# A two-layer diffusion block with routed experts: four edits between the output projection and the first expert

## The chip, the cores and the metric

The kernel runs on one core of one Trainium2 chip. The metric is the device time of one execution, in microseconds (us); the time before is the median of three runs. Engine names in this text: PE is TensorE's matmul side and PEld its weight loads, DVE is VectorE, ACT is ScalarE, POOL is GpSimd, SP is the queue that issues nearly all DMAs.

## The reference, cut to what matters

256 latent tokens `x` and 256 context tokens `ctx`, 1024 wide, pass two layers. Each layer has mixers whose merged result goes through one output projection, and then a mixture of 16 experts in which every expert takes its 32 best tokens per stream:

```python
x = x + g1 * merge_branches(attn_x, conv_x, pool_x, gate_x, lp)      # ends with  (...) @ lp['w_out']
x = x + g2 * expert_choice_ffn(modulate(rmsnorm(x, norm2_g[l]), sh2, sc2), w_router[l], w_e_gate[l], ...)
# expert_choice_ffn, per stream:
aff = softmax(h @ w_router)                      # (N, 16)
g, idx = top_k(aff.T, 32)                        # each expert's 32 tokens
xe = h[idx]
ye = (silu(xe @ w_gate) * (xe @ w_up)) @ w_down * g
out = zeros.at[idx].add(ye)
```

In layer 0 both streams go through the experts (64 tokens an expert), in layer 1 only `x` does (32 tokens an expert). The experts' weights are fp32, 12.6 MB an expert, 16 experts, two layers: some 400 MB of the 530 MB that the kernel reads.

## The kernel before

Everything is traced by the tile framework: the program is a list of instructions in Python order, and a planner reorders them by priority, readiness and estimated cost into one fixed instruction list for each engine. Each engine then runs its list strictly in order, so an instruction that waits holds all those behind it.

**The output projection**, `project(s)` (L846 on), for stream `s`: two halves `nh` of 512 output columns. For each half two PSUM banks, `pss[0]` and `pss[1]`, one for each 128 tokens (`t`). The weights come in four quarters `k2`; `split` (L229 on) makes a high part on ACT (L238) and a low part (L239: on POOL in layer 0, on DVE in layer 1), in one of two `ws` buffers. A quarter is 12 products (L872): three steps `st` (high x high, low x high weights, high x low weights), two `kk`, two `t`. After the last quarter, for each `t`, DVE multiplies by the gate (`tmp`, L877), the residual addition into `XS` follows (L879: on POOL for `nh` 1, `t` 0, otherwise on DVE), and ACT takes the squares (L880).

**The router**, `route(s)` (L884 on), a generator that is advanced in pieces. It turns `XS` into columns by PE transposes (L895), four to a bank, copies the bank out (L899 on ACT or L901 on DVE, in turn), multiplies by the router weights (L904), then comes the serial part: logits (L912 to L921), softmax, 32 best by four rounds of maximum and replace on DVE (L942, L943), slots, and the 0/1 selection matrix `S` (L965, L968), made for the last stream in chunks of four experts. Its first half of transposes needs only the projection's first column half and runs within the second.

**The gather**, `gather(s, parts)` (L979 on): for each of 8 column blocks `d` two fp32 products (L987) of `XS` (128 x 128, the weights of the array) with `S` (32 columns for each expert of the part), and an evacuation on DVE or ACT (L994, L992). Each product stands in the trace as two matmuls and two weight loads. In layer 0 `gather(0, 1)` is one part for stream 0 and overlaps `route(1)`; `gather(NS - 1, 4)` serves the last stream in four parts of four experts, of which the first runs ahead of expert 0.

**The experts** (L1033 on): for each of 16, gate and up products (L1080) in four steps `i`, then SiLU and product (L1085, L1087), then 8 or 16 steps of the gather of a later part (L1090), transposes (L1095), the down products (L1103 in layer 0, L1108 in layer 1), and every 4th (layer 0) or 2nd (layer 1) expert the scatter (L1125).

**The weights' stream**: SP issues the expert weights in pieces of 2 MB (L355) in a fixed order into slots (`order`). Each slot carries an older tile, and the DMA waits until that tile was last read. In layer 1 the first 11 entries hold expert 0 and most of expert 1. Of these the pieces in the memory of the projection's weight buffers are issued as the projection ends, the half piece in `xc` is issued when expert 0's step 0 was read, and the piece in `W01` after these when expert 1's step 0 was read. In layer 0 four entries are taken out of the later part of the order (`del order[77:81]`).

Of the kernel before, what the change touches and what calls it, by code (L numbers as in the profile page):

```python
# [121 lines left out]
def paired(c):  # L122

    return slice(256 * (c // 2) + c % 2, 256 * (c // 2) + 256, 2)
# [3 lines left out]
def dit_block(ctx: ExitStack, tc: tile.TileContext, out, kcv, kb16, rope_in, tok, cols, w_mod0, w_mod,  # L128
# [16 lines left out]
    def bank(tag, dt=F32):  # L145
        pool, bufs = psum[tag]
        return pool.tile([128, 512], dt, tag=tag, name=tag, bufs=bufs)
# [19 lines left out]
    def t2(name, n=512, dt=F32):  # L167
        return L.tile([128, n], dt, tag="t2", name=name, bufs=6)
# [42 lines left out]
    for l in range(DEPTH):  # L211
# [634 lines left out]
        def project(s):  # L846
            ssq[s] = small([128, 2, 2], "ssq")
            gbs = []
            for nh in range(2):
                gb = t2("gb")  # L850
                rr = 32 * nh + 16 * s
                pg = bank("ax")
                nc.tensor.matmul(pg, ident[:, rr:rr + 1].to_broadcast([128, 128]), GM[l], start=True,
                                 stop=True)
                nc.scalar.activation(gb, pg, AF.Copy)
                gbs.append(gb)
            for nh in range(2):
                pss = [bank("mm"), bank("mm")]
                for k2 in range(4):
                    if k2 % 2 == 0:  # L860
                        wo = load(w_out[l, nh, k2 // 2], "p (k n) -> p k n", k=4)
                    ws = split(wo[:, 2 * (k2 % 2):2 * (k2 % 2) + 2, :], "p (k n) -> p k n",
                               LOW["wout"][l], k=2)
                    wh, wl = [v.rearrange("p (k n) -> p k n", k=2) for v in ws]
                    for st in range(3):
                        for kk in range(2):
                            k = 2 * k2 + kk
                            for t in range(2):
                                tok = slice(256 * s + 128 * t, 256 * s + 128 * t + 128)
                                a = (mh, ml, mh)[st][:, k, tok]  # L870
                                b = (wh, wh, wl)[st][:, kk, :]
                                nc.tensor.matmul(pss[t], a, b, start=k == 0 and st == 0,  # L872
                                                 stop=k == 7 and st == 2)
                    yield
                for t in range(2):
                    tmp = t2("tmp")
                    nc.vector.tensor_mul(tmp, pss[t], gbs[nh])  # L877
                    xs = XS[s][:, t, nh * 512:(nh + 1) * 512]
                    (nc.gpsimd if nh == 1 and t == 0 else nc.vector).tensor_add(xs, xs, tmp)  # L879
                    nc.scalar.activation(t2("junk", 512, BF16), xs, AF.Square,  # L880
                                         accum_out=ssq[s][:, nh, t:t + 1])
                yield

        def route(s):  # L884
            pl = bank("ax")
            for d in range(8):
                nc.tensor.matmul(pl[32 * (d % 4):32 * (d % 4) + 32, 256:384], wr[:, d, :],
                                 modT[l][:, 1, s, 8 + d:9 + d].to_broadcast([128, 128]),
                                 start=d < 4, stop=d >= 4)
            for d2 in range(4):  # L890
                pt = bank("ax")
                for dd in range(2):
                    for t in range(2):
                        d = 2 * d2 + dd
                        nc.tensor.transpose(pt[:, dd * 256 + t * 128:dd * 256 + t * 128 + 128],  # L895
                                            XS[s][:, t, paired(d)], ident)
                xT = t2("xT")
                if d2 % 2:
                    nc.scalar.activation(xT, pt, AF.Copy)  # L899
                else:  # L900
                    nc.vector.tensor_copy(xT, pt)  # L901
                for dd in range(2):
                    d = 2 * d2 + dd
                    nc.tensor.matmul(pl[32 * (d % 4):32 * (d % 4) + 32, 0:256], wra[:, s, d, :],  # L904
                                     xT[:, dd * 256:dd * 256 + 256], start=d < 4, stop=d >= 4)
                if d2 % 2:
                    yield
            ss = small([128, 2], "ss")
            nc.gpsimd.tensor_add(ss, ssq[s][:, 0], ssq[s][:, 1])
            r = rms_scale(ss, 2)  # L910
# [65 lines left out]
            yield  # L976


        def gather(s, parts):  # L979
            ne = NE // parts  # L980
            for part in range(parts):
                es = slice(ne * part, ne * part + ne)
                for d in range(8):
                    px = bank("mm")[:, :32 * ne]
                    for t in range(2):
# [27 lines left out]
            pass  # L1013
        if NS == 2:
            xeT = [big(q, "xeT").rearrange("p (k e c) -> p k e c", k=4, e=NE) for q in "CD"]
            ga = gather(0, 1)
            for _ in rt1:
                next(ga, None)
                next(ga, None)
            for _ in ga:  # L1020
                pass
        else:
            xe = big("C", "xeT").rearrange("p (k e c) -> p k e c", k=8, e=NE)
            xeT = [xe[:, 0:4], xe[:, 4:8]]
        ga = gather(NS - 1, 4)
        for _ in range(8):
            next(ga)

# [4 lines left out]
        for e in range(NE):  # L1033
# [49 lines left out]
            for f in range(nb):  # L1083
# [2 lines left out]
                hm = t2("hm")  # L1086
                nc.vector.tensor_mul(hm[0:64, :], si[0:64, :], pgu[f][64:128, :])  # L1087
                hs.append(hm)
            for _ in range(8 if e == 0 or NS == 2 else 16):
                next(ga, None)  # L1090
            pt = bank("ax")
            for f in range(nb):
# [107 lines left out]
```

## Time and profile before

| | |
|---|---|
| median of 3 runs | 1712.94 us (1711.73 to 1713.78) |
| the profiled execution's own time | 1712.34 us |
| its span, first to last instruction | 1710.5 us |
| PE busy | 1483.2 us, 87% |
| DVE busy | 670.3 us, 39% |
| ACT busy | 407.6 us, 24% |
| POOL busy | 232.4 us, 14% |
| DMA, mean | 310 GB/s, 530 MB |

The profile is of one execution. Its page gives the span in 40 slices of 42.76 us with the rate of the DMAs in each; a rate near 428 GB/s is the highest that any long stretch reaches. "Granted clock" is the share of TensorE's 2.4 GHz: 1.00 is 2.4 GHz and 0.50 is 1.2 GHz. "Idle before <- X" in a row of the timeline is how long the engine stood before this instruction, and what ended the wait.

### The profile page before, as it was taken

Reading aid. Unit: us, or ns where it says so; the run is one execution under the profiler, and the core shown is the slowest. Engines: PE = TensorE matmul, PEld = TensorE weight load, DVE = VectorE, ACT = ScalarE, POOL = GpSimd, SP = SyncE. Lnnn points to the kernel's source line nnn. Section 1 sums busy time; section 2 is a strip of 40 time slices with the busy share of each in tenths; the row PEclk is TensorE's granted clock in tenths of the full one; section 3 lists DMA queues with packets and bytes.
Section 4 is the critical chain, followed back from the end, with each engine's and each line's share of the span. In section 5 each row is a group of like instructions: output and inputs, shape, how many; then the busy total and the mean of one; then the engine's idle time right before and its main releaser. Section 6 shows DMA issues by size and latency. Waiting matters only on the chain. (4 is left out here: it accounts for less than half of the span.)

```text
span 1710.5 us, 19121 instructions
## 1 busy us (share of the span) xinstructions
PE 1483.2 (87%) x7788; PEld 802.1 (47%) x7788; DVE 670.3 (39%) x1137; ACT 407.6 (24%) x760; POOL 232.4 (14%) x234
## 2 busy tenths in 40 slices
PE   6999989999999999999998899999979765666575
PEld 3665667888654433333332267789844111111111
DVE  3568993352553221121211268975542110111011
ACT  3455312232432100000000257434421000000001
POOL 0300430154740000000000020325100000000000
PEclk9999999999999999999999999999989887878878
DMA  9643435234546999999999865566689999999996
GB/s 398 230 173 130 148 144 207 75 139 181 197 176 255 425 428 427 428 426 428 428 407 428 334 242 179 196 225 229 268 336 429 427 429 427 428 427 428 428 428 258
DMA packets 48185, 530.01 MB, mean 310 GB/s; under 512 B 5345, under 2 KB 6113, under 8 KB 7906
## 3 DMA queue, kind: packets, MB, share of 16 engines
q1 hardware_dynamic: 46224, 526.10, 75.8%
q10 hardware_dynamic: 1874, 2.70, 0.5%
q8 instruction: 61, 1.00, 0.2%
q14 instruction: 26, 0.21, 0.0%
HBM read 527.73 MB, written 1.05 MB: 309 GB/s over the span
## 5 line engine op out<-in xcount | busy, mean ns | idle before, releaser
L1080 PE MATMUL mm<-we,xeT 128*32 128x512 f32 (+1 forms) x1880 | 347.1, 662 | 97.8 <-DMA we<-in_w_e_dram 97.8
L1080 PEld LDWEIGHTS mm<-we,xeT 128*32 128x32 f32 (+1 forms) x1880 | 95.1, 129 | 337.5 <-issue 190.2
L496 PE MATMUL mm<-hh,ws 128*128 128x512 f32 (+1 forms) x672 | 221.8, 349 | 0.3
L497 PE MATMUL mm<-hl,ws 128*128 128x512 f32 (+1 forms) x672 | 218.6, 344 | 0.5 <-DVE hl L430 0.4
L238 ACT ACTIVATE ws<-w 128x1024 fp32r<-128x1024 f32 x132 | 139.3, 1058 | 303.6 <-PE mm L499 202.5
L1087 DVE TENSOR_TENSOR hm<-si,mm 64x512 f32<-64x512 f32 x48 | 33.1, 690 | 405.8 <-ACT si L1085 271.4
L1085 ACT ACTIVATE si<-mm 64x512 f32<-64x512 f32 x48 | 28.3, 590 | 684.9 <-PE mm L1080 684.9
L478 DVE SCALAR_TENSOR_TENSOR acc<-up,dw,acc 128x512 f32<-128x512 f32 (+1 forms) x240 | 156.7, 693 | 1.1
L239 DVE TENSOR_TENSOR ws<-w,ws 128x1024 fp32r<-128x1024 f32 x94 | 122.3, 1304 | 70.5 <-ACT ws L238 70.2
L496 PEld LDWEIGHTS mm<-hh,ws 128*128 128x128 f32 x672 | 127.3, 190 | 29.2 <-issue 12.6
L497 PEld LDWEIGHTS mm<-hl,ws 128*128 128x128 f32 x672 | 127.4, 190 | 18.6 <-issue 3.5
L499 PE MATMUL mm<-hh,ws 128*128 128x512 f32 (+1 forms) x672 | 132.7, 339 | 1.0 <-DVE ws L239 0.9
L239 POOL TENSOR_TENSOR ws<-w,ws 128x1024 fp32r<-128x1024 f32 x38 | 97.2, 2564 | 211.2 <-ACT ws L238 211.2
L1103 PE MATMUL mm<-we,hT 128*64 128x512 f32 x432 | 111.2, 639 | 5.0 <-ACT hT L1098 4.8
L499 PEld LDWEIGHTS mm<-hh,ws 128*128 128x128 f32 x672 | 107.1, 189 | 15.9 <-DVE ws L239 2.1
L1045 POOL COPY sel<-kc 48x128 f32<-48x128 f32 (+1 forms) x16 | 4.6, 285 | 799.8 <-DVE hm L1087 428.8
L1115 DVE TENSOR_TENSOR Y<-mm,G 32x512 f32<-32x512 f32 x64 | 44.0, 687 | 135.8 <-PE mm L1103 135.0
L1108 PE MATMUL mm<-we,hT 128*32 128x512 f32 x424 | 69.1, 762 | 11.6 <-DMA we<-in_w_e_dram 9.6
L1103 PEld LDWEIGHTS mm<-we,hT 128*64 128x64 f32 x432 | 33.5, 146 | 76.5 <-issue 66.1
L1125 PE MATMUL ax<-Y,sg 128*128 128x512 f32 x128 | 58.4, 603 | 8.8 <-DVE Y L1118 6.4
L1118 DVE TENSOR_TENSOR Y<-mm,G 64x512 f32<-64x512 f32 x32 | 22.0, 688 | 96.1 <-PE mm L1108 95.7
L1095 PE MATMUL ax<-kc,hm 64*128 64x64 f32 x192 | 32.6, 294 | 31.0 <-DVE hm L1087 30.2
(260 smaller groups left out, 1715.3 us busy)
## 6 DMA issues: line engine op xcount, KB each, us to landing
we<-in_w_e_dram SPq DMA_DIRECT2D x166, 2048.0 KB, 26.6
w<-in_w_mod_dram SPq DMA_DIRECT2D x44, 1024.0 KB, 5.3
w<-in_w_in_dram SPq DMA_DIRECT2D x42, 1024.0 KB, 4.9
A<-in_w_e_dram SPq DMA_DIRECT2D x20, 2048.0 KB, 23.2
w<-in_w_out_dram SPq DMA_DIRECT2D x12, 1024.0 KB, 4.9
we<-in_w_e_dram SPq DMA_DIRECT2D x10, 1024.0 KB, 17.3
wm<-in_w_mod_dram SPq DMA_DIRECT2D x4, 1024.0 KB, 18.0
w<-in_w_attn_o_dram SPq DMA_DIRECT2D x4, 1024.0 KB, 4.9
```

The costliest lines, as they stand in the source:

```text
L238: nc.scalar.activation(h, src, AF.Copy)
L239: (nc.gpsimd if eng == "p" else nc.vector).tensor_sub(lw, src, h.bitcast(F32))
L478: nc.vector.scalar_tensor_tensor(acc[:, ch], up[:, ch, :, k:k + 256], dw[:, 4 * k + ch:4 * k + ch + 1], acc[:, ch], op0=ALU.mult, op1=ALU.add)
L496: nc.tensor.matmul(ps, wh[:, k, :], ah[:, k, :n], start=k == 0, stop=False)
L497: nc.tensor.matmul(ps, wh[:, k, :], al[:, k, :n], start=False, stop=False)
L499: nc.tensor.matmul(ps, wl[:, k, :], ah[:, k, :n], start=False, stop=k == nk - 1)
L1080: nc.tensor.matmul(o, xeT[k // 4][:, k % 4, e, :], w[:, kk, 512 * f:512 * f + 512], start=k == 0, stop=k == 7)
L1087: nc.vector.tensor_mul(hm[0:64, :], si[0:64, :], pgu[f][64:128, :])
L1103: nc.tensor.matmul(pd[64 * h:64 * h + 64, :], hT[:, 64 * k:64 * k + 64], rhs, start=k == 0, stop=k == 7)
L1108: nc.tensor.matmul(pd[o:o + 32, :], hT[:, c0:c0 + 32], rhs, start=k < 2, stop=k >= 6)
L1115: nc.vector.tensor_mul(Y[b0:b0 + 32, s, cols], pd[rw, :], G2[l][rw, :])
L1125: nc.tensor.matmul(po, sgs[s][:, t * 128:(t + 1) * 128], Y[:, s, cols], start=True, stop=True)
```

## The change

Four edits. In the projection's last quarter (`k2` 3) the 12 products are sorted by `t`, so that all six of `t` 0 come before the six of `t` 1. The addition L879 is on DVE in every case. The router's transposes are made in two halves of four column blocks, within a half by `t` first, into two banks, whose copies go to DVE and to ACT. And the last stream's gather is cut 2, 2, 4, 4, 4 experts instead of 4, 4, 4, 4; in layer 1 expert 0 now advances it by 16 steps instead of 8.

```diff
--- before.py
+++ after.py
@@ -862,21 +862,21 @@
                     ws = split(wo[:, 2 * (k2 % 2):2 * (k2 % 2) + 2, :], "p (k n) -> p k n",
                                LOW["wout"][l], k=2)
                     wh, wl = [v.rearrange("p (k n) -> p k n", k=2) for v in ws]
-                    for st in range(3):
-                        for kk in range(2):
-                            k = 2 * k2 + kk
-                            for t in range(2):
-                                tok = slice(256 * s + 128 * t, 256 * s + 128 * t + 128)
-                                a = (mh, ml, mh)[st][:, k, tok]
-                                b = (wh, wh, wl)[st][:, kk, :]
-                                nc.tensor.matmul(pss[t], a, b, start=k == 0 and st == 0,
-                                                 stop=k == 7 and st == 2)
+                    steps = [(st, kk, t) for st in range(3) for kk in range(2) for t in range(2)]
+                    if k2 == 3:
+
+                        steps.sort(key=lambda q: q[2])
+                    for st, kk, t in steps:
+                        k = 2 * k2 + kk
+                        tok = slice(256 * s + 128 * t, 256 * s + 128 * t + 128)
+                        nc.tensor.matmul(pss[t], (mh, ml, mh)[st][:, k, tok], (wh, wh, wl)[st][:, kk, :],
+                                         start=k == 0 and st == 0, stop=k == 7 and st == 2)
                     yield
                 for t in range(2):
                     tmp = t2("tmp")
                     nc.vector.tensor_mul(tmp, pss[t], gbs[nh])
                     xs = XS[s][:, t, nh * 512:(nh + 1) * 512]
-                    (nc.gpsimd if nh == 1 and t == 0 else nc.vector).tensor_add(xs, xs, tmp)
+                    nc.vector.tensor_add(xs, xs, tmp)
                     nc.scalar.activation(t2("junk", 512, BF16), xs, AF.Square,
                                          accum_out=ssq[s][:, nh, t:t + 1])
                 yield
@@ -887,24 +887,22 @@
                 nc.tensor.matmul(pl[32 * (d % 4):32 * (d % 4) + 32, 256:384], wr[:, d, :],
                                  modT[l][:, 1, s, 8 + d:9 + d].to_broadcast([128, 128]),
                                  start=d < 4, stop=d >= 4)
-            for d2 in range(4):
-                pt = bank("ax")
-                for dd in range(2):
-                    for t in range(2):
-                        d = 2 * d2 + dd
-                        nc.tensor.transpose(pt[:, dd * 256 + t * 128:dd * 256 + t * 128 + 128],
-                                            XS[s][:, t, paired(d)], ident)
-                xT = t2("xT")
-                if d2 % 2:
-                    nc.scalar.activation(xT, pt, AF.Copy)
-                else:
-                    nc.vector.tensor_copy(xT, pt)
-                for dd in range(2):
-                    d = 2 * d2 + dd
-                    nc.tensor.matmul(pl[32 * (d % 4):32 * (d % 4) + 32, 0:256], wra[:, s, d, :],
-                                     xT[:, dd * 256:dd * 256 + 256], start=d < 4, stop=d >= 4)
-                if d2 % 2:
-                    yield
+            for h in range(2):
+
+                pts = [bank("ax"), bank("ax")]
+                for t in range(2):
+                    for dd in range(4):
+                        o = 256 * (dd % 2) + 128 * t
+                        nc.tensor.transpose(pts[dd // 2][:, o:o + 128], XS[s][:, t, paired(4 * h + dd)],
+                                            ident)
+                xT = [t2("xT"), t2("xT")]
+                nc.vector.tensor_copy(xT[0], pts[0])
+                nc.scalar.activation(xT[1], pts[1], AF.Copy)
+                for dd in range(4):
+                    nc.tensor.matmul(pl[32 * dd:32 * dd + 32, 0:256], wra[:, s, 4 * h + dd, :],
+                                     xT[dd // 2][:, 256 * (dd % 2):256 * (dd % 2) + 256],
+                                     start=h == 0, stop=h == 1)
+                yield
             ss = small([128, 2], "ss")
             nc.gpsimd.tensor_add(ss, ssq[s][:, 0], ssq[s][:, 1])
             r = rms_scale(ss, 2)
@@ -976,10 +974,11 @@
             yield
 
 
-        def gather(s, parts):
-            ne = NE // parts
-            for part in range(parts):
-                es = slice(ne * part, ne * part + ne)
+        def gather(s, sizes):
+            e0 = 0
+            for ne in sizes:
+                es = slice(e0, e0 + ne)
+                e0 += ne
                 for d in range(8):
                     px = bank("mm")[:, :32 * ne]
                     for t in range(2):
@@ -1013,7 +1012,7 @@
             pass
         if NS == 2:
             xeT = [big(q, "xeT").rearrange("p (k e c) -> p k e c", k=4, e=NE) for q in "CD"]
-            ga = gather(0, 1)
+            ga = gather(0, (16,))
             for _ in rt1:
                 next(ga, None)
                 next(ga, None)
@@ -1022,7 +1021,7 @@
         else:
             xe = big("C", "xeT").rearrange("p (k e c) -> p k e c", k=8, e=NE)
             xeT = [xe[:, 0:4], xe[:, 4:8]]
-        ga = gather(NS - 1, 4)
+        ga = gather(NS - 1, (2, 2, 4, 4, 4))
         for _ in range(8):
             next(ga)
 
@@ -1086,7 +1085,7 @@
                 hm = t2("hm")
                 nc.vector.tensor_mul(hm[0:64, :], si[0:64, :], pgu[f][64:128, :])
                 hs.append(hm)
-            for _ in range(8 if e == 0 or NS == 2 else 16):
+            for _ in range(8 if NS == 2 else 16):
                 next(ga, None)
             pt = bank("ax")
             for f in range(nb):
```

## Rows read from the trace of the kernel before

**Rows 1.** The page: GB/s moved by DMA in the 40 slices.

```profile
GB/s 398 230 173 130 148 144 207 75 139 181 197 176 255 425 428 427 428 426 428 428 407 428 334 242 179 196 225 229 268 336 429 427 429 427 428 427 428 428 428 258
```

**Rows 2.** The chain of work that ended last: start, us, what.

```profile
1339.66 39.37 DMA we<-in_w_e_dram
```

**Rows 3.** Windows: stretch, length, busy PE PEld DVE ACT POOL, clock, DMA share, GB/s.

```profile
1268.00:1272.00 4.00, 4.00 (x44) 1.22 (x40) 0.00 (x0) 0.00 (x0) 0.00 (x0) 1.00 0.45 129
1284.00:1288.00 4.00, 4.00 (x44) 1.27 (x40) 0.00 (x0) 0.00 (x0) 0.00 (x0) 1.00 1.01 434
```

**Rows 4.** Timeline of SP's issues, layer 1: start, us, what.

```profile
1269.17 0.33 SPq L355 DMA_DIRECT2D we<-in_w_e_dram  x1
...
1285.56 0.33 SPq L355 DMA_DIRECT2D we<-in_w_e_dram  x1
```

**Rows 5.** Timeline, layer 1, from the projection's end to the router's products.

```profile
1242.94 1.07 PE L872 MATMUL mm<-ws,ml 128*128 128x512 f32 x4
1243.85 1.07 PE L872 MATMUL mm<-ws,mh 128*128 128x512 f32 x4
1244.73 1.29 DVE L877 TENSOR_TENSOR tmp<-mm,gb 128x512 f32<-128x512 f32 x2 [2.91 <-PE mm L872]
1245.50 1.26 POOL L879 TENSOR_TENSOR xr<-xr,tmp 128x512 f32<-128x512 f32 x1 [24.88 <-DVE tmp L877]
1246.05 1.26 DVE L879 TENSOR_TENSOR xr<-xr,tmp 128x512 f32<-128x512 f32 x1
...
1248.39 0.60 ACT L899 ACTIVATE xT<-ax 128x512 f32<-128x512 f32 x1 [0.26 <-PE ax L895]
1248.78 1.33 PE L904 MATMUL ax<-xT,rt 128*32 128x256 f32 x8 [0.42 <-DVE xT L901]
```

**Rows 6.** Gather and 64-column transposes at both clocks (timeline; windows as Rows 3).

```profile
518.68 4.04 PE L987 MATMUL mm<-S,xc 128*128 128x128 f32 x32 [1.32 <-ACT S L968]
...
1260.00:1264.00 4.00, 3.42 (x15) 2.93 (x16) 2.63 (x11) 2.90 (x9) 0.00 (x0) 0.50 1.04 446
1261.10 6.17 PE L987 MATMUL mm<-S,xr 128*128 128x128 f32 x32 [0.58 <-ACT S L968]
1278.47 0.55 PEld L1095 LDWEIGHTS ax<-kc,hm 64*128 64x128 f32 x4
...
1481.00:1482.00 1.00, 0.39 (x3) 0.39 (x4) 0.56 (x1) 0.00 (x0) 0.00 (x0) 0.50 1.00 426
1481.61 0.55 PEld L1095 LDWEIGHTS ax<-kc,hm 64*128 64x128 f32 x4 [3.21 <-DVE hm L1087]
```

**Rows 7.** Layer 0: two issues of SP, one PE wait, one window as Rows 3.

```profile
553.32 0.33 SPq L355 DMA_DIRECT2D we<-in_w_e_dram  x1
...
833.19 3.65 PE L1080 MATMUL mm<-we,xeT 128*64 128x512 f32 x16 [0.87 <-DMA we<-in_w_e_dram]
...
878.22 0.33 SPq L355 DMA_DIRECT2D we<-in_w_e_dram  x1
880.00:888.00 8.00, 8.00 (x40) 2.70 (x38) 2.74 (x4) 0.00 (x0) 0.00 (x0) 1.00 0.95 360
```

**Rows 8.** Layer 0, expert 3 (no gather beside it): timeline of PE.

```profile
618.71 1.48 PE L1095 MATMUL ax<-kc,hm 64*128 64x64 f32 x8 [0.63 <-DVE hm L1087]
620.94 5.25 PE L1103 MATMUL mm<-A,hT 128*64 128x512 f32 x16 [0.75 <-ACT hT L1098]
626.02 3.60 PE L1103 MATMUL mm<-we,hT 128*64 128x512 f32 x16
```

**Rows 9.** Layer 0, projection to gather: timeline, L879 (min/median/max ns), window as Rows 3.

```profile
L879 DVE TENSOR_TENSOR xr<-xr,tmp x6: 692/976/2249, 451.4 to 1246.1; 128x512 f32<-128x512 f32 x6
...
495.43 2.40 POOL L239 TENSOR_TENSOR ws<-w,ws 128x1024 fp32r<-128x1024 f32 x1 [3.00 <-ACT ws L238]
497.66 1.07 PE L872 MATMUL mm<-ws,ml 128*128 128x512 f32 x4
499.60:518.70 19.10, 17.39 (x62) 7.67 (x60) 12.94 (x37) 6.05 (x13) 2.37 (x4) 1.00 0.50 208
```

## The prediction

> **What bounds the kernel now.** I read the page's strip of DMA rates first. From slice 13 to 21 and again from slice 30 on it stands at 407 to 430 GB/s, which is all that these engines move [rows 1]: through most of both expert stages the kernel waits for weights. The chain of waits says the same, as its last third is one transfer after the other [rows 2]. So an edit that makes the router or the first gather shorter pays only if it moves the moment from which the weights stream without a break. I therefore looked for the last break in each layer, and for the release that ends it.
>
> Layer 1: the stream stands still around 1270, where 129 of 428 GB/s were moved in 4 us, a loss of 4 x (1 - 129/428) = 2.8 us [rows 3]. It resumes when expert 0's first step frees a half slot at 1269.17 [rows 4]; counted as full rate from 1270.8 on, an issue takes 1.65 us to become traffic. Four transfers of 7.3 MB follow. At 417 to 428 GB/s they last to about 1288.1. The next one waits for expert 1's first step and is issued at 1285.56 [rows 4], so it counts from 1287.2: in time, with some 0.9 us to spare, and the window there is full at 434 [rows 3].
>
> Layer 0: the stream is continuous from the issue at 553.32 (expert 1's first step). One later break stands out: the window 880 to 888 moved 360 GB/s, after an issue that a down product of PE released at 878.22 [rows 7]. That is a loss of 8 x (1 - 360/428) = 1.3 us. Until then PE ran from 520 on with one wait for weights, 0.87 us at 833 [rows 7]. At that place PE sets the stream, not the other way round.
>
> **Part by part.**
>
> *Last quarter by token halves.* It adds no product. Four products take 0.91 us (1242.94 to 1243.85 [rows 5]), one 0.23. With `t` 0 first its bank is ready 6 x 0.23 = 1.4 us before the end, where now it is one product before. Three costs. The low part of the weights is needed after four products, not eight, 0.9 us earlier. In layer 0 POOL finishes it at 495.43 + 2.40 = 497.83, and it would be wanted at 497.66 [rows 9], so PE stalls 0.2 us there. In layer 1 DVE makes it in half that time and I cost it at nothing; without that cover it is at most 0.9. And the last product that reads `ml` comes two products later, which delays the first transfers after the projection by 0.45 us; the later release (below) hides that.
>
> *Additions on DVE.* In layer 1 the serial tail now is: products end 1244.92, two gate products 1.29, POOL's addition 1.26 from 1245.50, DVE's stretched to 1.26 beside it until 1247.31, copies to 1248.99, router products 1.33 from 1248.78 to 1250.11 [rows 5]. After: `t` 0 is multiplied and added (0.65 + 0.69) inside the cover of the six products of `t` 1. Then 0.65 + 0.69 for `t` 1, to about 1246.4; four transposes, 0.7; the two copies side by side behind ACT's squares, to 1248.0; router products 0.64 at full clock, to 1248.6. That is 1.5 us earlier, with bounds of 0.7 (additions alone) and 2.0. The gain on POOL is nothing, since POOL is idle there.
>
> In layer 0 the same addition meets POOL at work on splits of the next stream at the end of `project(0)`: DVE's L879 took 692 ns alone and up to 2249 beside POOL [rows 9]. POOL's addition takes 1.26 and keeps the splits away while it runs. Two serial additions of up to 2.2 delay `route(0)`, behind whose steps PE's list holds `project(1)`: 0 to 1 us, I take 0.4. At the end of `project(1)` no split is left and the gain is as in layer 1, but the path then shares PE with 32 long matmuls of `gather(0)`. PE is busy 17.39 of the 19.10 us from there to the first gather of stream 1 [rows 9], so at most 1.7 us can go; I take 1.0, with bounds of 0 and 1.7.
>
> *Transposes by halves.* The same 16 transposes and four copies for each stream; its gain is in the tail above. Both copies of a half now stand together, so two `ax` banks and two `xT` buffers are held at a time. Of four and six that is room enough, and I cost it at nothing, or 0.7 (one copy) if a bank is missing.
>
> *First gather for two experts.* This is the disputed price, since no 64-column gather is in the trace. At full clock a part of four takes 4.04 us for 32 loads and 32 matmuls, 0.126 a pair; at half clock 6.17 in layer 1, mostly 0.21 a pair [rows 6]. If columns set the pace, a half part takes half. If the load of 128 weight columns does, nothing is won at full clock. The nearest rows are L1095's: loads of 128 columns beside matmuls of 64, four in 0.55 us at full clock and four in 0.55 at half clock [rows 6], 0.12 to 0.14 each. So I take 32 x 0.12 + 0.15 = 4.0 us for a part of two at either clock. Layer 0 wins 0 to 0.3 (0.2), layer 1 wins 2.2 on the first part. The price is a fifth part of 4.0 us on PE.
>
> The Trainium skill, "TensorE: Matmul & The Clock Gate", section "LDWEIGHTS (loading the stationary operand)", gives the load as columns / 1.2 ns whatever the rows, 107 ns for 128; by that a part of two could not go under 32 x 0.107 = 3.4 us, and the rows above sit a little over it.
>
> *Where the fifth part lands, layer 1.* Expert 0 now pulls two parts (4.0 + 4.1) before its down products instead of one (4.1). Expert 1's first step, which ends the stream's next wait, moves by -1.5 (tail) - 2.2 (first part) + 4.0 (extra part) + 0 to 1.2 (2.35 us of expert 0's products at half clock, as the first part no longer outlasts the slow stretch) = +0.3 to +1.5, middle +0.9. The break at 1270 does close: step 0 ends some 3 us earlier. But the stream, 2.3 us ahead, then stands at `W01`: its shift is -0.9 + 0.9 = 0, with bounds of -1.2 and +0.7. The gain is given back one slot later. I take -0.1.
>
> *Where it lands, layer 0.* Expert 1's first step comes G = 1.0 + 0.2 - 0.4 = 0.8 us earlier, and so does the stream. Expert 3 now carries a part that it did not have: +4.1 on PE. It fills a stall of 0.63 and may save the slow stretch that followed, 5.25 against 3.60 for the same 16 matmuls, 1.65 [rows 8]. So the net is +1.8 to +3.5; I take 2.3, near the lower end, since the part keeps PE busy just where it fell idle. PE had 0.87 of waiting at 833 to absorb it. The release at 878 moves by -0.8 + 2.3 - 0.87 = +0.6, with bounds of -1.1 (G of 2.0, the stretch saved) and +3.6 (G of -1.0, the stretch kept).
>
> The sum on the profiled execution, 1712.34: +0.6 - 0.1 = +0.5, so 1712.8. The median of the runs lies 0.6 above that execution: **1713.4 us**.
>
> **The rivals.**
>
> *Columns set the gather's pace.* Then the first two parts of layer 0 take 2.0 us each and the total gather work stays what it was. The release at 878 then moves by -1.0 + 0.4 - (0.6 to 2.3 saved in expert 3) - 0.87, some -2.9. In layer 1 expert 1's step moves by -1.5 - 3.1 + 2.0 + 0.5 = -2.1, and the stream wins all of 2.3. Sum -5.2: **1707.7**. For it speaks only that the half-clock part was paced by columns; against it L1095's rows, the same at both clocks.
>
> The same page of the Trainium skill has a rule for this side in "Back-to-back issue gap": N / 2.4 + 2.5 ns for an isolated stream, 29 ns at 64 columns, which would halve the gather; L1095's 0.12 to 0.14 us for 64 columns speaks against its use here.
>
> *The lists fall well.* The planner's new order lets `project(1)` end 1.5 us earlier (against the 0.4 later that I take), the tail of layer 0 gives its full 1.7, and expert 3's slow stretch is saved: G is 3.4, layer 0 -3.4 + 1.8 - 0.87 = -2.5, layer 1 -1.0. Sum -3.5: **1709.4**.
>
> *Slower: DVE's additions beside POOL's splits.* If both additions of `project(0)` meet a split (from some 3 us of overlap on this decides), `route(0)` comes 1.5 to 2.5 us later, PE's list waits behind it, and `project(1)` ends 2 us later. With the tail's 1.0 and 0.2 G is -0.8. Expert 3 keeps its slow stretch, +3.5. Layer 0: +0.8 + 3.5 - 0.87 = +3.4, layer 1 +0.4. Sum +3.8: **1716.7**. For it: 2249 ns in rows of this very line. Against it: the earlier start of `t` 0 may let its addition pass between two splits.
>
> **How the numbers follow.** About 0.2%, 3.4 us, is what a measurement of this kernel can tell from no change: 1709.5 to 1716.4. No change to speak of (1710.5 to 1715.8): 0.68. Columns: 0.07. Lists fall well: 0.12, half of it beyond the bound. Slower by additions and the extra part: 0.13, most of it beyond. So faster 0.14, same 0.74, slower 0.12. The range reaches into the rivals on both sides: 1708.6 to 1716.8.
>
> **What would show it.** Part of two: a first L987 group of 3.8 to 4.2 us in both layers; one of 2.0 to 2.5 makes the column rival right. Tail: 1.2 to 1.8 us less between the last L872 and L904 in layer 1, and no L879 on POOL. Break at 1270 gone, and a new one of 1 to 2.5 us where SP waits for expert 1's step near 1286: without it layer 1 gains up to 2.3 and I am wrong there. Layer 0: L879 on DVE near 466 at 2.2 us, expert 3 with an L987 group, and SP's late release near 878 later relative to 553. What I can't see from here is the planner's new order of each engine's list. If it moves the gather's extra part behind expert 0's down products, or the stream's issues, the sum changes by up to 3 us either way.

## The result

The changed kernel takes **1727.08 us** (median of 4 runs, 1723.45 to 1727.87) against 1713.36 for the kernel before beside it: a ratio of **1.0077, 95% interval 1.0056 to 1.0098**. It is 13.7 us slower. The forecast was 1713.4, with a range up to 1716.8 and a chance of 0.12 for slower.

The profiled execution has a span of 1724.5 us, 14.1 more than before. The products of layer 1's projection begin at 1220.00 before and at 1230.04 after: layer 0 costs 10.0 us, layer 1 another 4.0.

First the strips of the page after: granted clock in tenths, and the rate of the DMAs. In slice 12 (517 to 561 us here, 513 to 556 before) the rate is 185 GB/s, where before it was 255 [rows 1]; in slice 30 it is 390, where before it was 429.

```profile
PEclk9999999999998999999999999999979878887778
...
GB/s 397 227 171 129 147 150 198 88 154 161 184 174 185 428 428 428 427 427 429 426 407 430 352 251 176 177 232 237 266 335 390 429 426 430 426 429 426 429 426 263
```

PE around the first experts of layer 0, timeline of the kernel after (start, us, line, operation, matmuls in the row, wait before):

```profile
520.75 5.16 PE L986 MATMUL mm<-S,xc 128*128 128x64 f32 x32 [1.32 <-ACT S L966]
525.85 15.99 PE L1079 MATMUL mm<-we,xeT 128*64 128x512 f32 x64
541.77 4.12 PE L986 MATMUL mm<-S,xc 128*128 128x64 f32 x28
545.82 0.57 PE L1094 MATMUL ax<-kc,hm 64*128 64x64 f32 x3
546.32 0.69 PE L986 MATMUL mm<-S,xc 128*128 128x64 f32 x4
546.93 0.86 PE L1094 MATMUL ax<-kc,hm 64*128 64x64 f32 x5
548.53 6.29 PE L1102 MATMUL mm<-A,hT 128*64 128x512 f32 x16 [0.74 <-ACT hT L1097]
554.65 3.60 PE L1102 MATMUL mm<-we,hT 128*64 128x512 f32 x16
558.09 4.46 PE L1079 MATMUL mm<-we,xeT 128*64 128x512 f32 x20
```

And the same stretches as windows (busy PE, PEld, DVE, ACT, POOL, then the granted clock, DMA share, GB/s):

```profile
520.00:523.00 3.00, 2.25 (x19) 2.25 (x20) 2.31 (x10) 2.70 (x10) 0.00 (x0) 1.00 0.00 0
523.00:527.00 4.00, 4.00 (x19) 3.26 (x20) 0.69 (x2) 1.14 (x4) 0.00 (x0) 0.52 0.00 0
527.00:530.00 3.00, 3.00 (x8) 0.71 (x6) 0.00 (x0) 0.00 (x0) 0.00 (x0) 0.50 0.00 0
...
546.00:550.00 4.00, 3.25 (x16) 2.00 (x18) 0.27 (x1) 1.00 (x2) 0.00 (x0) 0.63 0.49 209
550.00:554.00 4.00, 4.00 (x12) 1.18 (x10) 0.00 (x0) 0.00 (x0) 0.00 (x0) 0.52 0.00 0
554.00:558.00 4.00, 4.00 (x20) 1.26 (x18) 0.00 (x0) 0.00 (x0) 0.00 (x0) 1.00 0.55 143
```

Read the two together. The first part of two begins at 2.4 GHz, and PE has no wait from 520.75 on; yet from 523.2 the clock is 1.2 GHz, and expert 0's first products run at that. The part takes 5.16 us, where the part of four took 4.04 [rows 6]. The second part ends the same way: at 547.0, as its last products run and with no wait of PE since 520.75, the clock falls again, and 16 down products take 6.29 us, while the next 16 take 3.60. Expert 1 starts at 558.09, before at 549.68. In the last column the weights' stream stands at 0 from 550 to 554; finer windows have 16 GB/s from 549 on and nothing until 555.

SP's list shows why it stopped so long. Three pieces go out, and the next entry is the load into slot A, which waits for the slow down products; the entry behind it had its slot free from about 542 on (in `e3_piece_order`, below, that piece goes out at 542.15):

```profile
531.58 7.20 SPq L355 DMA_DIRECT2D we<-in_w_e_dram  x3
554.87 0.33 SPq L355 DMA_DIRECT2D A<-in_w_e_dram  x1
555.24 6.82 SPq L355 DMA_DIRECT2D we<-in_w_e_dram  x2
```

Before, a fourth piece was issued at 536.64, ahead of slot A's load at 546.46. The planner exchanged the two entries.

In layer 1, PE's timeline and windows of the kernel after:

```profile
1269.17 7.09 PE L986 MATMUL mm<-S,xr 128*128 128x64 f32 x32 [0.57 <-ACT S L966]
1276.19 1.06 PE L1079 MATMUL mm<-we,xeT 128*32 128x512 f32 x1
...
1285.52 2.75 PE L986 MATMUL mm<-S,xr 128*128 128x64 f32 x20
1288.70 5.45 PE L986 MATMUL mm<-S,xr 128*128 128x64 f32 x44 [0.44 <-DVE xeT L993]
```

```profile
1272.00:1276.00 4.00, 4.00 (x20) 4.00 (x20) 1.03 (x3) 0.81 (x2) 0.00 (x0) 0.50 0.97 418
1276.00:1280.00 4.00, 4.00 (x22) 1.07 (x25) 0.00 (x0) 0.40 (x1) 0.00 (x0) 0.50 0.62 254
1280.00:1284.00 4.00, 4.00 (x36) 1.04 (x32) 0.00 (x0) 0.00 (x0) 0.00 (x0) 0.89 0.79 268
...
1296.00:1300.00 4.00, 4.00 (x40) 1.17 (x36) 0.48 (x1) 0.31 (x1) 0.00 (x0) 1.00 0.75 311
1300.00:1304.00 4.00, 4.00 (x44) 1.23 (x40) 0.00 (x0) 0.00 (x0) 0.00 (x0) 1.00 0.49 127
```

The half part takes 7.09 us, more than the whole part's 6.17 [rows 6]: 20 loads fill 4.00 us at 1.2 GHz, 0.2 each, and loads (PEld) are as busy as products. At that clock a pair takes 0.213 us from start to start in both kernels; the whole part was shorter because the clock came back at 1265.9, 4.8 us after it began. Here PE is without a wait from 1269.17, but the clock comes back only at 1280.9, well into expert 0's products. Against 428 GB/s the four windows with low rates lost 1.6 + 1.5 + 1.1 + 2.8 = 7.0 us of stream, where before the break at 1270 lost 2.8 [rows 3]. The difference, 4.2, is the 4.0 us of layer 1.

### The profile page after: what moved, and what is told of

Same layout as the page of the kernel before. It is cut to its first block, busy times and chain, and to the rows that moved or that the text cites. A ratio compares the mean times of both kernels' runs of the same rounds, so it can differ in the third digit from the quotient of the medians.

```text
span 1724.5 us, 19262 instructions
## 1 busy us (share of the span) xinstructions
PE 1501.4 (87%) x7852; PEld 813.4 (47%) x7852; DVE 675.4 (39%) x1148; ACT 410.9 (24%) x768; POOL 226.3 (13%) x231
## 5 line engine op out<-in xcount | busy, mean ns | idle before, releaser
L1079 PE MATMUL mm<-we,xeT 128*32 128x512 f32 (+1 forms) x1880 | 352.0, 668 | 95.1 <-DMA we<-in_w_e_dram 95.1
L1094 PE MATMUL ax<-kc,hm 64*128 64x64 f32 x192 | 32.6, 297 | 30.3 <-DVE hm L1086 29.8
```

What stands on the lines that cost most here:

```text
L1079: nc.tensor.matmul(o, xeT[k // 4][:, k % 4, e, :], w[:, kk, 512 * f:512 * f + 512], start=k == 0, stop=k == 7)
```

## The experiments

The theory after this reading: products of 64 columns behind weight loads of 128 are no shorter than those of 128 columns, **and they bring the array's clock down or keep it down**, so that the expert's products behind them run at half speed. Rivals: SP's exchanged entries; the additions on DVE and the planner's new lists around the projection; the fifth part by itself. Each comparison is with runs of the kernel before on the same chip, in five rounds. The times are medians; the ratio comes from all the runs and is not that of the medians. `e1` to `e4` ran on one chip, `e5` to `e7`, `e8` and `e9`, and `e10` to `e12` on three others, on which the kernel before had medians of 1713.18, 1714.29, 1712.92 and 1713.56; between two groups only distances from the kernel before are compared.

| kernel | us | against before (95%) | projection of layer 1 begins | from there to the end of the span |
|---|---|---|---|---|
| before (profile) | | | 1220.00 | 490.5 |
| after | 1727.08 | 1.0077 (1.0056 to 1.0098) | 1230.04 | 494.5 |
| `e1_no_fifth` | 1711.84 | 0.9985 (0.9973 to 0.9998) | 1221.35 | 489.5 |
| `e2_fifth_in_layer1` | 1719.19 | 1.0029 (1.0017 to 1.0040) | 1222.29 | 496.8 |
| `e3_piece_order` | 1722.98 | 1.0049 (1.0032 to 1.0067) | 1227.47 | 494.3 |
| `e4_full_columns` | 1712.29 | 0.9994 (0.9983 to 1.0005) | 1218.94 | 491.1 |
| `e5_full_columns_layer0` | 1710.15 | 0.9979 (0.9970 to 0.9989) | 1219.60 | 489.2 |
| `e6_pool_addition_kept` | 1711.09 | 0.9989 (0.9980 to 0.9999) | 1221.48 | 489.6 |
| `e7_warm_before_narrow` | 1716.74 | 1.0010 (0.9999 to 1.0020) | 1220.60 | 495.1 |
| `e8_fifth_wide_alone` | 1711.99 | 0.9991 (0.9982 to 0.9999) | 1219.27 | 490.6 |
| `e9_old_transposes` | 1710.99 | 0.9985 (0.9976 to 0.9995) | 1222.12 | 489.3 |
| `e10_changed_beside` | 1725.79 | 1.0075 (1.0063 to 1.0088) | 1228.23 | 494.3 |
| `e11_piece_order_beside` | 1722.28 | 1.0048 (1.0036 to 1.0060) | 1224.73 | 495.6 |
| `e12_narrow_layer0` | 1717.22 | 1.0021 (1.0008 to 1.0034) | 1227.11 | 490.3 |

### Without the fourth edit

```diff
-        ga = gather(NS - 1, (2, 2, 4, 4, 4))
+        ga = gather(NS - 1, (4, 4, 4, 4))
...
-            for _ in range(8 if NS == 2 else 16):
+            for _ in range(8 if e == 0 or NS == 2 else 16):
```

> The change without its fourth edit: the last stream's gather is again 4, 4, 4, 4 experts, the other three edits stay. Theory 'narrow parts' (the two parts of 64 columns cost more than parts of 128, and the array falls to 1.2 GHz after them): most of the 13.7 us is gone; what is left is layer 0's projection, which ended 2.6 us later, against a tail that is some 2 us shorter in layer 1 and pays nothing because of the next release: 1712 to 1716. Rival 'projection and router' (additions on DVE beside POOL's splits, transposes by halves, and the planner's new lists from them): 1722 to 1727. No slow stretch of the clock at the first experts of layer 0 by the first theory.

1711.84 us: the whole loss is gone, and 0.15% is won. The fourth edit holds all of it; the rival around the projection falls.

### The fourth edit in one layer

```diff
-        ga = gather(NS - 1, (2, 2, 4, 4, 4))
+        ga = gather(NS - 1, (4, 4, 4, 4) if NS == 2 else (2, 2, 4, 4, 4))
```

> The whole change, but the gather of layer 0 stays at four parts of four; only layer 1 has 2, 2, 4, 4, 4. Theory 'narrow parts': layer 0 costs as much as without the fourth edit, layer 1 adds the 4 us that it adds in the changed kernel: 3 to 5 us over the run without the fourth edit, 1716 to 1720. Rival 'everything is in layer 0' (layer 1 hides it behind the weights): the same time as without the fourth edit, within 1 us.

1719.19: 7.4 us over `e1_no_fifth`, more than the 3 to 5 expected. Layer 1 hides nothing of it. This profile has one slow stretch more than that of the changed kernel, inside the second narrow part. PE's one wait there is 0.44 us, at 1280.48, and the clock falls at 1282.1; 44 products take 6.97 us, where the changed kernel's took 5.45:

```profile
1278.00:1280.00 2.00, 2.00 (x16) 1.80 (x15) 0.69 (x2) 1.94 (x4) 0.00 (x0) 1.00 1.01 410
1280.00:1284.00 4.00, 3.56 (x23) 3.52 (x23) 1.79 (x4) 0.94 (x3) 0.00 (x0) 0.76 0.99 420
```

For layer 0 the tuple is the other way round, and SP's entries are put back as in the next experiment:

> The three first edits, five parts with two of 64 columns in layer 0 alone, four parts in layer 1, and SP's order as in the kernel before. It isolates what narrow parts cost in layer 0. If the costs add up (1711.8 without the fourth edit, 6.1 us between the traces with and without narrow parts at layer 1's start): 1716 to 1719. Rival 'the expert stage of layer 0 takes the delay back before layer 1': within 2 us of 1711.8.

1717.22: 3.7 us over the kernel before beside it, where `e1_no_fifth` was 1.3 under its own, so 5.0 us for the fourth edit in layer 0. The fourth edit with its narrow parts costs 5 to 7 us in each layer. The median hides a spread: three of these twelve runs took 1712.5 to 1712.9, the others 1714.7 to 1719.8. What differs in the three is not known, since only a run of 1719.43 has a profile.

### SP's two entries

```diff
-                    nc.sync.dma_start(v, w_e[l, e, i, :, o:o + n_])
+                    with tc.high_priority(60) if not last and nload[0] == 16 else nullcontext(): nc.sync.dma_start(v, w_e[l, e, i, :, o:o + n_])
```

> The changed kernel with one thing else: in layer 0 the load of one 2 MB piece stands again ahead of the load into slot A on SP's list, as in the kernel before; the lists of PE, DVE, ACT and POOL are the same as in the changed kernel, instruction for instruction. Theory 'narrow parts': PE reaches expert 1 some 8 us late anyhow, and only the part of the stream's lag beyond that (10.9 against 8.4 us) comes back: 1723.5 to 1726. Rival 'SP's order' (the piece that now waits 13 us behind slot A's release is the cause in layer 0): 1717 to 1721.

Four pieces are issued ahead of slot A's load again (timeline of SP, this kernel). The edit moves the piece one place further forward than it stood before, ahead of the third one too, so that these two go out at 542.15 and 542.52; the stream hardly feels that, as the window from 542 to 546 still has 369 GB/s, a loss of 4 x (1 - 369/428) = 0.6 us:

```profile
531.85 11.11 SPq L355 DMA_DIRECT2D we<-in_w_e_dram  x4
555.30 0.33 SPq L355 DMA_DIRECT2D A<-in_w_e_dram  x1
```

1722.98 is 9.8 us over the kernel before beside it, 3.9 less than the changed kernel was; it lies a little below what the first theory gave (1723.5 to 1726) and above the rival's 1717 to 1721. The two were then run side by side:

> The changed kernel as it is, beside the two that follow on one chip, so that the price of SP's order is read between kernels timed together. Theory 'narrow parts, and SP's order on top': 1726 to 1728, 2.5 to 5 us over the next run. Rival 'SP's order costs nothing by itself': within 1.5 us of it.

> The changed kernel with the one 2 MB piece put back ahead of slot A's load on SP's list, nothing else. 1722 to 1724.5 by the first theory; as the run before it by the rival.

1725.79 and 1722.28: the exchanged entries cost 3.5 us by the medians (4.4 by the means), about a quarter of the loss. `e10_changed_beside` also shows that the fall of the clock is not certain at each narrow part. In that profile the first part kept the clock at 1.00 and took 4.17 us; the second one ended in a slow stretch, as in all five profiles with narrow parts in layer 0.

```profile
521.00 4.17 PE L986 MATMUL mm<-S,xc 128*128 128x64 f32 x32 [1.32 <-ACT S L966]
...
545.75 6.40 PE L1102 MATMUL mm<-A,hT 128*64 128x512 f32 x16 [0.75 <-ACT hT L1097]
```

### Same parts, full columns

```diff
-                    px = bank("mm")[:, :32 * ne]
+                    pw, ws = (bank("mm")[:, :32 * max(4, ne)], slice(0, 4) if ne == 2 else es)
                     for t in range(2):
-                        Sv = St[s][:, t, es].rearrange("p e c -> p (e c)")
-                        nc.tensor.matmul(px, XS[s][:, t, paired(d)], Sv, start=t == 0, stop=t == 1)
-                    pxv = px.rearrange("p (e c) -> p e c", e=ne)
+                        Sv = St[s][:, t, ws].rearrange("p e c -> p (e c)")
+                        nc.tensor.matmul(pw, XS[s][:, t, paired(d)], Sv, start=t == 0, stop=t == 1)
+                    pxv = pw[:, 32 * (es.start - ws.start):32 * (es.stop - ws.start)].rearrange("p (e c) -> p e c", e=ne)
```

> The changed kernel, but the first two parts of the gather are computed over all four experts of their chunk (128 columns, of which 64 are evacuated). The number of parts, loads and products is that of the changed kernel, and SP's list is that of the kernel before. Theory 'narrow parts lower the clock': with 128 columns a part takes 4.0 us in layer 0 and 6.2 in layer 1 as before, no slow stretch follows at 523 and 547, expert 0 of layer 1 starts near full clock; it remains the fifth part (about 2 us in layer 0, 2 in layer 1) and the projection's 2: 1716 to 1721, under the run with the piece order by 4 us or more. Rival 'the fifth part itself and the order': the same time as the run with the piece order, within 1 us, and the slow stretches stay.

This is the experiment that decides. PE does twice the columns in the first two parts, and the kernel takes 1712.29 us, 10.7 under `e3_piece_order`. SP's list is that of the kernel before; against `e3_piece_order` it differs by the one place told of above, worth 0.6 us. PE's timeline of this kernel:

```profile
519.01 4.04 PE L986 MATMUL mm<-S,xc 128*128 128x128 f32 x32 [1.32 <-ACT S L966]
522.98 13.95 PE L1079 MATMUL mm<-we,xeT 128*64 128x512 f32 x64
536.86 4.33 PE L986 MATMUL mm<-S,xc 128*128 128x128 f32 x32
541.12 1.17 PE L1094 MATMUL ax<-kc,hm 64*128 64x64 f32 x8
543.04 3.65 PE L1102 MATMUL mm<-A,hT 128*64 128x512 f32 x16 [0.75 <-ACT hT L1097]
...
1258.07 6.28 PE L986 MATMUL mm<-S,xr 128*128 128x128 f32 x32 [0.58 <-ACT S L966]
1264.28 0.62 PE L1079 MATMUL mm<-we,xeT 128*32 128x512 f32 x1
```

The windows from 520 to 554 all stand at clock 1.00:

```profile
520.00:523.00 3.00, 3.00 (x28) 2.88 (x27) 1.37 (x4) 2.01 (x7) 0.00 (x0) 1.00 0.00 0
523.00:527.00 4.00, 4.00 (x21) 1.43 (x22) 0.00 (x0) 0.41 (x1) 0.00 (x0) 1.00 0.00 0
...
550.00:554.00 4.00, 4.00 (x22) 1.39 (x20) 2.74 (x4) 0.00 (x0) 0.00 (x0) 1.00 0.82 348
```

The loads and the parts are the same; the columns are changed, and with them the slow stretches at 523 and 547 go, and in layer 1 the first of expert 0's products takes 0.62 us, not 1.06. One thing more differs in the profiles: this one lacks the slow stretch at 479, far ahead of the gather, which that of `e3_piece_order` has and which is worth some 1.9 us (see the account of layer 0 below). It can't make up the 10.7. I had expected 1716 to 1721, since I still charged the fifth part about 2 us in each layer and the projection 2.

### A warm array ahead of a narrow part

```diff
-            wk = t2("wk", 256)
+            wk = t2("wk", 256); wm_ = t2("sel", 128); last and nc.scalar.activation(wm_, ident, AF.Copy, scale=sm[:, 0:1]); [nc.tensor.matmul(bank("mm"), wm_, XS[0][:, 0, 0:512], start=True, stop=True) for _ in range(3 if last else 0)]
```

> The run with the fifth part in layer 1 alone (1719.2 us), and there three extra products of 128x512 on PE, read by nobody, while DVE finds the 32 best and PE would stand idle for 4.4 us. Theory 'narrow parts lower the clock by themselves': even if the gather of 64 columns starts at 2.4 GHz, the clock falls some 2 to 3 us into it as in layer 0, and expert 0 starts at 1.2 GHz: 1718 to 1721. Rival 'they only fail to end the slow stretch that the router's wait began': the first part takes 3.8 us, expert 0 runs at 2.4 GHz, 1713 to 1716. If the extra products do not lift the clock by the time of the gather (0.50 there), the run tells the two apart only in part.

In layer 1 one could still say that the narrow part only fails to end the slow stretch which the router's wait began. Here the part starts at 1259.83 at 2.4 GHz. Timeline of PE and windows:

```profile
1252.98 4.26 PE L936 MATMUL mm<-xr,sel 128*128 128x512 f32 x6
...
1259.83 6.26 PE L986 MATMUL mm<-S,xr 128*128 128x64 f32 x32 [1.20 <-ACT S L966]
1266.01 1.06 PE L1079 MATMUL mm<-we,xeT 128*32 128x512 f32 x1
```

```profile
1258.00:1260.00 2.00, 0.71 (x7) 0.39 (x6) 1.56 (x8) 0.63 (x3) 0.00 (x0) 1.00 1.05 451
1260.00:1262.00 2.00, 2.00 (x14) 2.00 (x15) 1.18 (x6) 2.00 (x8) 0.00 (x0) 0.72 0.98 418
1262.00:1264.00 2.00, 2.00 (x12) 2.00 (x11) 0.54 (x2) 0.51 (x2) 0.00 (x0) 0.50 0.97 418
```

The clock falls at 1260.9, within the part, and stays at 1.2 GHz until 1271.1; expert 0 starts at 1.06 us a product. So the slow stretch of the router's wait isn't needed for expert 0 to start slow. That the part alone brought the clock down isn't shown here: PE had stood idle for 1.20 us just before and was busy 0.71 of the 2 us from 1258 on, and no run has full columns behind the same products. The fall in `e2_fifth_in_layer1` at 1282.1 is the clearer row for layer 1. The time, 1716.74, is 2.5 us over the kernel before beside it, where `e2_fifth_in_layer1` was 6.0 over its own. In the profiles the part took 6.26 us for 7.09, and the second slow stretch is missing. I had written 1718 to 1721.

### What the other three edits and the fifth part are worth

> The three first edits, and in layer 0 five parts of the gather of which the first two are computed over 128 columns (64 evacuated); layer 1 keeps four parts of four. Theory 'narrow parts': layer 0 as in the run with full columns, 1218.9 us to layer 1's projection, layer 1 as in the run without the fourth edit, 489.5 us from there: 1709 to 1711.5, the fifth part costing nothing in layer 0 since it fills the stall of expert 3. Rival 'a fifth part always costs its 4 us of PE': 1714 to 1716.

The three first edits, five parts with full columns in layer 0, four parts in layer 1 (edits as above): **1710.15 us, faster than both kernels**, by 0.21% (0.11 to 0.30) than the one before. The fifth part costs nothing that the times show: it stands where expert 3 had its stall, and the slow stretch of [rows 8] (5.25 us for the first 16 down products) is not there. Timeline of PE of this kernel:

```profile
619.91 4.04 PE L986 MATMUL mm<-S,xc 128*128 128x128 f32 x32
...
625.79 3.65 PE L1102 MATMUL mm<-A,hT 128*64 128x512 f32 x16 [0.75 <-ACT hT L1097]
```

> The kernel before with one thing new: in layer 0 the gather has five parts, the first two computed over 128 columns (64 evacuated). None of the other three edits. It tells what the 3 to 4 us come from that the run with the three edits and these five parts won. Theory 'the fifth part fills expert 3's stall': layer 0 is 1 to 2 us shorter than before (no slow stretch of the clock near 620), layer 1 as before: 1711 to 1713 beside a before of 1713 to 1714. Rival 'the other three edits won it': within 0.5 us of before, and the slow stretch near 620 stays.

The kernel before with that gather in layer 0 and nothing else takes 1711.99, a ratio of 0.9991: some 0.9 us won. The slow stretch near 620 is gone here too. Neither half alone is far beyond what can be told from no change.

> The first and the third edit alone: the gather is 4, 4, 4, 4, and the addition of nh 1, t 0 stays on POOL. Against the run without the fourth edit (1711.8) this prices the move of the addition to DVE. In layer 1 the stretch from the last projection product to the first gather product should be 0.7 to 1.3 us longer with POOL (1.26 us against 0.69, and DVE beside it stretched). Theory 'additions cost nothing that counts': the whole time within 1.5 us of 1711.8. Rival 'DVE's additions delay layer 0's router and projection': project(1) ends about 1 us earlier here and the time is 1710 or less.

```diff
-                    nc.vector.tensor_add(xs, xs, tmp)
+                    (nc.gpsimd if nh == 1 and t == 0 else nc.vector).tensor_add(xs, xs, tmp)
```

With the addition on POOL the ratio is 0.9989, with DVE (`e1_no_fifth`) 0.9985. In layer 1 it is 2.79 us here from the end of the last projection product, 1246.42, to the router's products, and 2.80 with DVE (to the first gather product 14.01 and 14.57). Rows of PE, first this kernel, then `e1_no_fifth`:

```profile
1247.19 1.48 PE L896 MATMUL ax<-kc,xr 128*128 128x128 f32 x8 [0.77 <-POOL xr L879]
1249.21 0.77 PE L902 MATMUL ax<-xT,rt 128*32 128x256 f32 x8 [0.54 <-DVE xT L899]
```

```profile
1246.44 0.75 PE L896 MATMUL ax<-kc,xr 128*128 128x128 f32 x4 [0.15 <-DVE xr L879]
1247.80 0.74 PE L896 MATMUL ax<-kc,xr 128*128 128x128 f32 x4 [0.61 <-DVE xr L879]
1249.09 0.77 PE L902 MATMUL ax<-xT,rt 128*32 128x256 f32 x8 [0.54 <-DVE xT L899]
```

POOL's 1.26 us run beside DVE's work for `t` 1, so the engine of that addition is of no account. My expectation of 0.7 to 1.3 us more was wrong.

> The first and the second edit, with the router's transposes and copies in the old order and the gather in four parts. From the last projection product to the first of the last eight router products layer 1 took 3.9 us before, 2.8 with the three edits and 2.8 with the addition left on POOL. Theory 'the products' order by token halves wins it': 2.8 to 3.1 here too. Rival 'the transposes by halves, with the two copies side by side, win it': 3.5 to 3.9. The time either way within 1.5 us of 1711.8, since the stream decides.

With the old transposes (the old loop over `d2`) the same distance is 2.92 us and the time 1710.99. Before it was 3.86 [rows 5]. So it is the order of the products by token halves that shortens the tail, by 0.9; the transposes add 0.1.

## Why the prediction was wrong

**The step that failed is the price of the first gather for two, and what the array does after it.** The text took 4.0 us for a part of two at either clock. At 2.4 GHz that is right: 4.17 us where the clock held (`e10_changed_beside`), from start to start 0.118 us a pair. At 1.2 GHz it is wrong: 0.213 us a pair, 7.09 us in layer 1. The nearest rows that I took, L1095's 0.55 us for four at both clocks [rows 6], are loads from 64 partitions; the row of the same line of code, the gather of 128 columns at half clock, 0.21 a pair, stood in the same group and was read as a pace of columns. The rival "columns set the pace" fell as well: at either clock a load with a product of 64 columns takes the time of one with 128.

**The larger part was not in the sum at all.** I let the clock depend on whether PE waits, and wrote of the part in expert 3 that it "keeps PE busy". In layer 0 the clock was to stay at 2.4 GHz; it fell at 523, 2.4 us into the first narrow part, and at 547, at the end of the second, while PE had no wait. In layer 1 I gave expert 0 at half clock 0 to 1.2 us; it ran slow for 4.7 us, and its gate and up products took 9.3 us. The full-column run shows the cause: with the columns changed and the waits the same, the slow stretches are gone. Why small products do this to the clock no run shows.

By terms, layer 1: the tail won 2.0 (forecast 1.5, bounds 0.7 to 2.0; in part luck, since from the projection's last product to the gather it took 16.18 us before, 14.20 after, and 15.38 in `e8_fifth_wide_alone`, which has none of the three edits); the first part cost 0.9 (forecast -2.2); from expert 0's first product to expert 1's it took 23.0 us for 16.4, +6.6 (forecast +4.0 to +5.2). Expert 1's first step came 5.6 us later, forecast +0.3 to +1.5. The mechanism was the one named, a break that moves from 1270 to `W01`: SP's issue there is at 1301.18, and the window around it has 127 GB/s. Its size was mis-set by 4.7, and the break at 1270 did not close.

Layer 0: `project(1)` ended 2.6 us later (forecast 0.4), the tail won 0.5 (forecast 1.0, bounds 0 to 1.7), the first part cost 1.1 (forecast -0.2), expert 0 took 32.2 us for 27.0 (forecast no change). Together expert 1 came 8.4 later, forecast 0.8 earlier. Of the 2.6, about 1.9 is another slow stretch of the clock, at 479: it shows in ten of the twelve profiles of kernels with the first edit, and `e3_piece_order` and `e11_piece_order_beside`, with the same lists on every engine, differ in it (502.37 against 500.51 for the end of `project(1)`). Before and in `e8_fifth_wide_alone`, without that edit, it is missing. Whether the edit brings it on, and how, is open.

**SP's order.** The text held the order of the issues fixed and named, at its end, up to 3 us if the planner moved them. It exchanged two, for 3.5 us. The bound was named but not put into the sum or the range; it is of that size because the entry waits behind slot A's release, and that release came 8 us late.

**The fifth part.** Its price in layer 0 was put at +2.3, at least 1.8. With full columns it is nothing or a little less than nothing (`e5_full_columns_layer0`, `e8_fifth_wide_alone`). In layer 1 it costs 1.6 us in the traces (491.1 against 489.5), where the forecast had -0.1 for that whole layer.

**The rest was right.** No L879 is on POOL, its DVE rows near 466 take 1.63 and 2.44 us in layer 0 (forecast 2.2), the tails are shorter by about what was said, and the three first edits change little together: 1711.84, 1.3 us under the kernel before beside it. But the text booked the shorter tail under the additions, and the runs show that it comes from the products' order, not from the engine of the additions. The slower rival, additions beside POOL's splits, is not what happened either. The chance of slower, 0.12, was too small because each case took PE's price from rows at a settled clock, and none let a smaller operation change the clock.

The sum as measured, each term from kernels on one chip or from distances to the kernel before: -1.3 (three edits), +5.0 (narrow parts in layer 0), +3.5 (SP's order), and the rest, 1727.1 - 1713.4 - 7.2 = +6.5 for layer 1, within the 5.1 (`e11_piece_order_beside` less `e12_narrow_layer0`) and 7.4 (`e2_fifth_in_layer1` less `e1_no_fifth`) that the runs give for it. Both layers' terms hold the fifth part too.

## What to carry to other kernels

Before an operation on PE is made smaller, ask whether its weight load sets its pace: if it does, fewer columns win no time and may lower the clock of everything behind it. Price a new shape from rows with the same number of partitions and at the clock that will be granted there, and add what follows at the other clock. And compare the order of the DMA queue after a change far from it: an entry that the planner moves behind a slow release costs a stretch of the stream.

## What the hardware showed

A PE that the rows show as busy without a wait lost its clock: in layer 0 of the changed kernel at 547.0, at the end of the second narrow part, when PE had not waited since 520.75. Shortly after a small wait it fell at 523.2 (a wait of 1.32 us, ended at 520.75) and in layer 1 of `e2_fifth_in_layer1` at 1282.1 (0.44 us, ended at 1280.48). Each time products of 64 columns behind loads of 128 columns were running or had just run. In layer 0 of `e4_full_columns`, with 128 columns, the same loads and the same wait of 1.32 us, the clock stayed at 1.00. Narrow products also left a low clock low: 7.09 us of them in layer 1 ended at 0.50, while 128-column products had it back after 4.8 us (1261.10 to 1265.9, the kernel before). Not each narrow part did it: the first of layer 0 in `e10_changed_beside` and the second of layer 1 in the changed kernel ran at 1.00 throughout. The Trainium skill, "TensorE: Matmul & The Clock Gate", section "HAM oscillation — how this bites in real kernels", puts the fall of the clock down to stretches in which PE waits for data. The fall at 547.0 came without such a wait.

Loads for the gather (128 partitions, 128 columns) step by 0.118 us at 2.4 GHz and 0.213 at 1.2 GHz, worked out from their start times; L1094's loads (64 partitions, 128 columns; L1095 in the kernel before) by 0.118 at both, though at 1.2 GHz only groups of four stand in the rows. The same page of the Trainium skill, section "LDWEIGHTS (loading the stationary operand)", lets only the columns count. At full clock the rows agree with that, at half clock they don't; whether the partitions, the short groups or something else in these products makes the difference was not tried.
